# Squares of all norms summed by products in four groups of columns, and x loaded two tiles of channels at a time

## The chip, the core and the metric

The kernel runs on one core of a Trainium2 chip. The metric is the device time of one execution in microseconds. A core has a matrix engine (TensorE, PE in the rows; its weight loads stand apart as PEld), a vector engine (VectorE, DVE), an engine for activations (ScalarE, ACT), a general one (GpSimd, POOL) and SyncE (SP), which issues all the loads and stores here. They run beside each other, each in the order of its own queue, and wait for one another through semaphores. TensorE writes to PSUM, which has eight banks of 128 x 512 floats. Its clock has two levels, 1.2 and 2.4 GHz; the profile shows which one was granted.

## What is computed

Two layers of a backbone over 1024 tokens of 1024 channels: first a convolution layer, then a pooling layer. Both begin with a root-mean-square norm whose result is scaled and shifted, and the first has a layer norm inside. Cut to what matters:

```python
def _rms(x, g):
    y = x * lax.rsqrt(jnp.mean(x * x, axis=-1, keepdims=True) + EPS)
    return y * g

def _conv_mixer(h, w_in, dw, db, ln_g, ln_b, w_out):
    a, b, g = jnp.split(h @ w_in, 3, axis=-1)
    y = a * sigmoid(b)
    y = depthwise_conv(y, dw, width=31) + db
    y = silu(_layernorm(y, ln_g, ln_b)) * silu(g)
    return y @ w_out

# layer 0: convolution mixer, layer 1: pooling mixer
h = _rms(x, norm_g[i]) * (1.0 + sc) + sh
x = x + gt * mixer(h)
```

sh, sc and gt come from the vector c by a product with w_mod.

## The kernel before

Everything is held with the channels on the 128 partitions and the tokens along the row, so a tensor of 1024 x 1024 is eight tiles of channels (KT = 8), each in two halves of 512 tokens (h = 0 and 1). The kernel goes half by half: layer 0 for half 0, then for half 1, with layer 1 of half 0 laid beside the second. All large products are made of three products of fp32r parts (`mm3`, lines 200 to 203: high by high, high by low, low by high), so every weight and every right-hand side is first split into a high part on ACT (line 164 or 165) and a low part on DVE or POOL (line 169 or 170).

There are six norms to which the change belongs: x0 and x1 (the input's two halves, lines 327 to 331), z0 and z1 (the layer norm inside the convolution mixer, `layernorm`, lines 529 to 546), y0 and y1 (the norm before layer 1, summed in `out_half` while it writes the residual, lines 575 to 604, and used in `h2_half`). A norm needs, for each token, the sum of the squares over all channels, which lie on the partitions. Two helpers do it:

- `squares` (line 252; x0, x1 and y1): ACT squares a tile, DVE adds it to a running total of 128 x 512 (line 266), and at the end TensorE takes each block of 128 tokens of the total as its stationary operand and streams one column of ones (line 234). For y1 the last tile of squares isn't added but summed by four products of its own.
- `square_sums` (line 270; z0, z1 and y0): ACT squares a tile, and TensorE takes each of its four blocks of 128 tokens as the stationary operand and streams one column of ones (line 277). The sums of all eight tiles accumulate in one bank, as four columns with the tokens on the partitions.

A tile of squares lives in a ring of two buffers (`sq`), so the third square waits until the first has been summed. `rstd_rows` (line 225) ends the norm: ACT scales the sums by 1/1024 and adds EPS (line 240), POOL raises to the power -0.5 (line 242), ACT makes four diagonal blocks (line 247) and TensorE spreads them over all partitions with a product of ones (line 248, tile `rb`). DVE then multiplies every tile by `rb`.

The convolution has 31 taps. For some tiles of channels DVE does it in PSUM (lines 480 to 489); for two tiles of half 0 and five of half 1 ACT multiplies (line 471, tile `pr`, a ring of two) and POOL adds (line 472).

The gate and modulation vectors of the later steps (`gemv`, line 291) are made by products with 32 columns of weights: four of them fill the four groups of 32 partitions of one bank and are in the array at the same time (line 299). Their result lies in rows 0, 32, 64 and 96 and is turned by a product with `sel`, a selection matrix of 128 x 4 (line 308).

Order: the tile framework lays out each engine's queue when the kernel is built, by a list schedule with priorities and a cost model of its own; `priority(-LATER)` puts work ahead, conv work stands behind, and `behind([...])` makes instructions of a block follow a given instruction in the order of that one's engine. Where a norm is awaited, some projection products are kept back behind the spread product (`HOLD`), so that TensorE has work meanwhile. In the first stage (lines 385 to 421) the loads go in one order by hand: x0 in eight loads, then for each of eight tiles two blocks of w_mod and one of the first weights; DVE takes the modulation from the w_mod blocks by dot products (line 287). They are placed behind `x_done`, the last instruction that `norm_x(0)` issues for the squares. `load_x` writes eight tiles of 128 x 512, two to a unit of 128 x 1024. `out_half` loads the same x again for the residual, in eight loads (line 579).

Of the kernel before, what the change touches and what calls it, by code (L numbers as in the profile page):

```python
# [14 lines left out]
P = 128  # L15
D = 1024
# [37 lines left out]
def hybrid_kernel(ctx, tc, xT, vecs, wm, wk, cv_first, cv_w, cv_wo, pl_w, pl_grp, pl_wo, out):  # L54
# [6 lines left out]
    RINGS = {"w": 4, "raw": 4, "sg": 2, "sq": 2, "pr": 2, "vs": 1}  # L61
# [37 lines left out]
    def hs(h):  # L99
        return slice(h * HW, (h + 1) * HW)  # L100
# [3 lines left out]

    def packed(tags, name):
        res = []
        for j, tag in enumerate(tags):
            u = unit(tag, f"{name}{j}")
            res += [u[:, hs(0)], u[:, hs(1)]]
        return res  # L110
# [114 lines left out]
    def rstd_rows(total, name):  # L225


        sums, vp = total
        if vp is None:
            vp = axps(f"vp{name}")  # L230
            with priority(-LATER):
                for i, summed in enumerate(sums):
                    for j in range(4):
                        nc.tensor.matmul(
                            vp[:, j : j + 1], summed[:, bl(j)], ones[:, 0:1], start=i + j == 0,
                            stop=i == len(sums) - 1, skip_group_check=True,
                        )
        ve = S.tile([P, 4], F32, tag="ve", name=f"ve{name}", bufs=2)
        with priority(-LATER):
            nc.scalar.activation(ve, vp[:, 0:4], AF.Identity, scale=1.0 / D, bias=eps)  # L240
        rs = S.tile([P, 4], F32, tag="vr", name=f"vr{name}", bufs=2)
        power_done[0] = nc.gpsimd.tensor_tensor(out=rs, in0=ve, in1=mhalf[:, 0:4], op=ALU.pow)  # L242
        rb = axps(f"rb{name}")
        dg = half("sq", f"dg{name}")
        with priority(-LATER):
            for j in range(4):
                spread = nc.scalar.activation(dg[:, bl(j)], ident, AF.Copy, scale=rs[:, j : j + 1])
            done = nc.tensor.matmul(rb, ones, dg, start=True, stop=True)  # L248
        spread_done[0] = spread
        return rb, done  # L250

    def squares(xs, name, apart=False):

        total = half("vs", f"va{name}")
        sums = [total]

        def add(i):
            if i == 0:
                nc.scalar.activation(total, xs[i], AF.Square)
                return None  # L260
            sq = half("sq", f"sq{name}{i}")
            nc.scalar.activation(sq, xs[i], AF.Square)
            if apart and i == KT - 1:
                sums.append(sq)
                return None
            return nc.vector.tensor_tensor(out=total, in0=total, in1=sq, op=ALU.add)

        return (sums, None), add

    def square_sums(xs, name, vp):  # L270


        def add(i):
            sq = half("sq", f"sq{name}{i}")
            done = nc.scalar.activation(sq, xs[i], AF.Square)  # L275
            for j in range(4):
                nc.tensor.matmul(  # L277
                    vp[:, j : j + 1], sq[:, bl(j)], ones[:, 0:1], start=i + j == 0, stop=i == KT - 1,
                    skip_group_check=True,
                )  # L280
            return done

        return (None, vp), add
# [38 lines left out]
    def load_x(h):  # L322
        xs[h] = packed([f"{'FZ'[h]}{j}" for j in range(4)], f"x{h}")
        for kt in range(KT):
            load_next(xs[h][kt], xT[bl(kt), hs(h)])

    def norm_x(h):
        total, add = squares(xs[h], f"x{h}")
# [246 lines left out]
    def out_half(h, y1, ws, done, beside=None):  # L575
        group = len(ws)
        x1 = packed([f"Z{j}" for j in range(4)], f"xr{h}")
        for m in range(KT):
            nc.sync.dma_start(out=x1[m], in_=xT[bl(m), hs(h)])
        total, add = squares(x1, f"y{h}", True) if h else square_sums(x1, f"y{h}", axps("vpy0"))  # L580
# [303 lines left out]
```

## Time and profile before

| | us |
|---|---|
| median of 3 runs | 758.52 (757.62 to 759.13) |
| the profiled execution | 758.71 |
| its span, from the first to the last instruction | 756.9 |
| PE busy | 724.2 (96%) |
| PEld busy | 574.1 (76%) |
| DVE busy | 532.1 (70%) |
| POOL busy | 435.4 (58%) |
| ACT busy | 386.4 (51%) |

All times in the rows are microseconds from the start of the span. A matmul's shown duration overlaps that of its neighbours, so the time that products take is read from start to start. Every fp32 matmul stands as two records, an fp32r one as one. A row of the timeline gives start, duration, engine, line, operation, output and inputs, shape and count, and in brackets how long the engine was idle before it and what ended that. Tile names have their buffer numbers left out: vpx, vpz and vpy are the sums of the squares, sqx, sqz and sqy the squares, rbx, rbz and rby the spread results.

### The profile page before, as it was taken

The numbers are of one execution on the slowest core, as the hardware profiler recorded it, in microseconds if no ns is written. First come the engines' busy times: TensorE is split into PE (matmuls) and PEld (weight loads), VectorE is DVE, ScalarE is ACT, GpSimd is POOL, SyncE is SP. The second block draws the span as 40 slices with busy tenths as digits, with TensorE's granted clock in tenths as the row PEclk, the third lists the DMA queues.
The fourth block names the chain that finished last, engine by engine and source line by source line (L and its number), as shares of the span: only waits on it lengthen the run. The fifth ranks groups of instructions, "written<-read, shape, count | busy, mean of one in ns | idle before, by whom it ended". The sixth has DMA issues, their size and how long they took to land.

```text
span 756.9 us, 9894 instructions
## 1 busy us (share of the span) xinstructions
PE 724.2 (96%) x3572; PEld 574.1 (76%) x3572; DVE 532.1 (70%) x724; ACT 386.4 (51%) x576; POOL 435.4 (58%) x377
## 2 busy tenths in 40 slices
PE   3899999999999999999989989999999999999998
PEld 1677786676768788778766768788888788888997
DVE  5997997889898941589969989671737364477321
ACT  5355556656613346876886676652414433334110
POOL 2000889999913438899998999763117413344232
PEclk9999999999999999999999989999999999999999
DMA  8882006466323441643650132445625610334132
GB/s 324 315 318 82 0 1 249 167 223 233 132 82 98 152 153 63 202 140 113 207 171 24 57 126 83 154 168 160 203 92 203 200 56 28 98 112 140 56 126 72
DMA packets 36481, 105.68 MB, mean 140 GB/s; under 512 B 4048, under 2 KB 6224, under 8 KB 36432
## 3 DMA queue, kind: packets, MB, share of 16 engines
q1 hardware_dynamic: 36432, 105.05, 40.8%
q8 instruction: 28, 0.46, 0.2%
q14 instruction: 21, 0.17, 0.1%
HBM read 92.45 MB, written 12.58 MB: 139 GB/s over the span
## 4 chain that ended last, share of the span: by engine, by line
PE 70%; DVE 14%; POOL 8%; ACT 3%; issue 2%; DMA 2%; SPq 0%; DVEq 0%; POOLq 0%; ACTq 0%
POOL z L472 8%; PE ps L201 4%; PE ps L203 4%; PE ps L202 4%; PE psf L202 4%; PE psf L203 4%; PE psf L201 4%; PE psv L203 3%; PE psv L202 3%; PE psv L201 3%; PE psq L202 3%; PE psq L201 3%; PE psq L203 3%; PE psg L203 3%; PE psg L201 3%; PE psg L202 3%
## 5 line engine op out<-in xcount | busy, mean ns | idle before, releaser
L472 POOL TENSOR_TENSOR z<-z,pr 128x512 f32<-128x512 f32 (+8 forms) x210 | 297.1, 1415 | 49.4 <-ACT pr L471 21.2
L471 ACT ACTIVATE pr<-y,VT 128x512 f32<-128x512 f32 (+8 forms) x210 | 150.2, 719 | 96.8 <-POOL z L472 90.2
L484 DVE SCALAR_TENSOR_TENSOR cv<-y,VT,cv 128x512 f32<-128x512 f32 (+12 forms) x261 | 175.4, 741 | 0.4
L770 DVE SCALAR_TENSOR_TENSOR xf<-psf,gt,xf 128x260 f32<-128x260 f32 (+1 forms) x24 | 13.2, 570 | 36.9 <-PE psf L203 31.4
L753 DVE SCALAR_TENSOR_TENSOR q<-psy,VT,q 128x260 f32<-128x260 f32 (+1 forms) x24 | 13.6, 571 | 31.9 <-PE psy L203 31.7
L242 POOL TENSOR_TENSOR vrx<-vex,mhalf 128x4 f32<-128x4 f32 x2 | 2.1, 1026 | 57.2 <-ACT vex L240 57.2
L567 DVE TENSOR_TENSOR z<-z,rbz 128x512 f32<-128x512 f32 x16 | 10.7, 680 | 28.9 <-PE rbz L248 28.9
L671 DVE TENSOR_TENSOR s<-v 128x535 f32<-128x535 f32 x8 | 12.3, 1536 | 19.5 <-ACT v L719 19.5
L675 DVE TENSOR_TENSOR s<-s 128x517 f32<-128x517 f32 (+5 forms) x24 | 20.9, 870 | 0.6
L559 ACT ACTIVATE gn<-z,VT 128x512 f32<-128x512 f32 x16 | 12.4, 777 | 14.6 <-DVE z L567 14.4
L287 DVE SCALAR_TENSOR_TENSOR wmb<-wmb,s_row 128x1024 f32<-128x1024 f32 x16 | 19.4, 1220 | 0.0
L583 DVE SCALAR_TENSOR_TENSOR xr<-pso,gt,xr 128x512 f32<-128x512 f32 x16 | 11.5, 741 | 10.7 <-PE pso L203 10.7
L299 PE MATMUL gv<-wk,srep 128*32 128x256 f32 x256 | 18.6, 388 | 0.0
L164 ACT CAST y<-q 128x504 fp32r<-128x504 f32 (+1 forms) x16 | 9.9, 618 | 16.8 <-DVE q L753 16.8
L169 DVE TENSOR_TENSOR y<-q,y 128x504 fp32r<-128x504 f32 (+1 forms) x16 | 13.9, 869 | 3.6 <-ACT y L164 3.6
L277 PEld LDWEIGHTS vpz<-ones,sqz 128*128 128x128 f32 x128 | 15.5, 191 | 0.7
L275 ACT ACTIVATE sqz<-z 128x512 f32<-128x512 f32 x16 | 9.8, 629 | 12.0 <-PE vpz L277 11.5
L202 PE MATMUL psy<-pd,grs 128*128 128x260 f32 (+1 forms) x48 | 15.3, 320 | 0.0
L203 PE MATMUL psy<-pd,grs 128*128 128x260 f32 (+1 forms) x48 | 15.3, 319 | 0.0
L201 PE MATMUL psy<-pd,grs 128*128 128x260 f32 (+1 forms) x48 | 15.1, 318 | 0.0
L277 PE MATMUL vpz<-ones,sqz 128*128 128x1 f32 x128 | 14.7, 245 | 0.0
L169 DVE TENSOR_TENSOR grs<-gr,grs 128x512 fp32r<-128x512 f32 x8 | 9.1, 1132 | 8.0 <-ACT grs L164 8.0
(2503 smaller groups left out, 2352.6 us busy)
## 6 DMA issues: line engine op xcount, KB each, us to landing
wk<-in_wk SPq DMA_DIRECT2D x32, 512.0 KB, 5.1
wmb<-in_wm SPq DMA_DIRECT2D x16, 512.0 KB, 6.4
wo<-in_cv_wo SPq DMA_DIRECT2D x16, 512.0 KB, 3.5
wp<-in_pl_wo SPq DMA_DIRECT2D x16, 512.0 KB, 3.5
wg<-in_cv_w SPq DMA_DIRECT2D x12, 512.0 KB, 3.7
wv<-in_pl_w SPq DMA_DIRECT2D x12, 512.0 KB, 3.4
wq<-in_pl_w SPq DMA_DIRECT2D x12, 512.0 KB, 3.5
x<-in_xT SPq DMA_DIRECT2D x16, 256.0 KB, 6.2
```

The source lines that it names most:

```text
L169: return eng.tensor_tensor(out=lo, in0=src, in1=hi.bitcast(F32), op=ALU.subtract)
L201: nc.tensor.matmul(ps, w[0], r[0], start=first, stop=False)
L202: nc.tensor.matmul(ps, w[0], r[1], start=False, stop=False)
L203: nc.tensor.matmul(ps, w[1], r[0], start=False, stop=last)
L277: nc.tensor.matmul(vp[:, j : j + 1], sq[:, bl(j)], ones[:, 0:1], start=i + j == 0, stop=i == KT - 1, skip_group_check=True,)
L287: nc.vector.scalar_tensor_tensor(out=w, in0=w, scalar=1.0, in1=s_row, op0=ALU.mult, op1=ALU.mult, accum_out=out)
L299: nc.tensor.matmul(ps[32 * q : 32 * q + 32, :256], srep[:, kt, :], w[:, 256 * q : 256 * q + 256], start=kt == 0, stop=kt == KT - 1,)
L471: nc.scalar.activation(pr[:, o], y[:, i], AF.Copy, scale=dw(k))
L472: nc.gpsimd.tensor_tensor(out=z[:, o], in0=z[:, o], in1=pr[:, o], op=ALU.add)
L484: nc.vector.scalar_tensor_tensor(out=a[:, o], in0=y[:, i], scalar=dw(k), in1=a[:, o], op0=ALU.mult, op1=ALU.add)
L675: nc.vector.tensor_tensor(out=s[:, :m], in0=s[:, :m], in1=s[:, step : step + m], op=ALU.add)
L753: mixed[0] = nc.vector.scalar_tensor_tensor(out=sg[m][:, piece], in0=ps, scalar=vcol(ct, V_PS), in1=sg[m][:, piece], op0=ALU.mult, op1=ALU ...
```

## The change

All six norms now use `square_sums`, and its products are turned round: for each of the four blocks of 128 tokens the stationary operand is 32 columns of `onesd` (all 1/1024) and the squares are streamed, 128 columns, into one of the four groups of 32 partitions (`token_sums`). The bank then holds, in each group, the mean of squares of 128 tokens along the row. `rstd_rows` copies this 128 x 128 block to SBUF on ACT with EPS added, turns it with a product with `sel` into four columns, copies these on ACT, and goes on as before; the power on POOL now stands inside the priority block. `squares`, its running total and the DVE adds are gone. What `norm_x` returns as the last instruction is now the last square on ACT, where it was the last add on DVE.

x is laid out anew in memory, so that one load of 128 rows of 4 KB brings two tiles of channels of one half: `load_x` and `out_half` make four loads of 512 KB each where they made eight of 256 KB.

```diff
-    def rstd_rows(total, name):
-        sums, vp = total
-        if vp is None:
-            vp = axps(f"vp{name}")
-            with priority(-LATER):
-                for i, summed in enumerate(sums):
-                    for j in range(4):
-                        nc.tensor.matmul(
-                            vp[:, j : j + 1], summed[:, bl(j)], ones[:, 0:1], start=i + j == 0,
-                            stop=i == len(sums) - 1, skip_group_check=True,
-                        )
-        ve = S.tile([P, 4], F32, tag="ve", name=f"ve{name}", bufs=2)
+    def token_sums(ps, src, first, last):
+        for j in range(4):
+            nc.tensor.matmul(ps[32 * j : 32 * j + 32, :P], onesd[:, :32], src[:, bl(j)], start=first, stop=last)
+
+    def rstd_rows(vp, name):
+        row = S.tile([P, P], F32, tag="vrow", name=f"vrow{name}", bufs=1)
+        rs = S.tile([P, 4], F32, tag="vr", name=f"vr{name}", bufs=2)
         with priority(-LATER):
-            nc.scalar.activation(ve, vp[:, 0:4], AF.Identity, scale=1.0 / D, bias=eps)
-        rs = S.tile([P, 4], F32, tag="vr", name=f"vr{name}", bufs=2)
-        power_done[0] = nc.gpsimd.tensor_tensor(out=rs, in0=ve, in1=mhalf[:, 0:4], op=ALU.pow)
+            nc.scalar.activation(row, vp[:, :P], AF.Identity, bias=eps)
+            nc.tensor.matmul(vp[:, P : P + 4], row, sel, start=True, stop=True)
+            ve = S.tile([P, 4], F32, tag="ve", name=f"ve{name}", bufs=2)
+            nc.scalar.copy(ve, vp[:, P : P + 4])
+            power_done[0] = nc.gpsimd.tensor_tensor(out=rs, in0=ve, in1=mhalf[:, 0:4], op=ALU.pow)
...
-    def squares(xs, name, apart=False):
...
     def square_sums(xs, name, vp):
         def add(i):
             sq = half("sq", f"sq{name}{i}")
             done = nc.scalar.activation(sq, xs[i], AF.Square)
-            for j in range(4):
-                nc.tensor.matmul(
-                    vp[:, j : j + 1], sq[:, bl(j)], ones[:, 0:1], start=i + j == 0, stop=i == KT - 1,
-                    skip_group_check=True,
-                )
+            token_sums(vp, sq, i == 0, i == KT - 1)
             return done
-        return (None, vp), add
+        return vp, add
...
     def load_x(h):
-        xs[h] = packed([f"{'FZ'[h]}{j}" for j in range(4)], f"x{h}")
-        for kt in range(KT):
-            load_next(xs[h][kt], xT[bl(kt), hs(h)])
+        xs[h] = []
+        for j in range(4):
+            u = unit(f"{'FZ'[h]}{j}", f"x{h}{j}")
+            load_next(u, xT[h, j])
+            xs[h] += [u[:, hs(0)], u[:, hs(1)]]
 
     def norm_x(h):
-        total, add = squares(xs[h], f"x{h}")
+        total, add = square_sums(xs[h], f"x{h}", axps(f"vpx{h}"))
...
     def out_half(h, y1, ws, done, beside=None):
-        x1 = packed([f"Z{j}" for j in range(4)], f"xr{h}")
-        for m in range(KT):
-            nc.sync.dma_start(out=x1[m], in_=xT[bl(m), hs(h)])
-        total, add = squares(x1, f"y{h}", True) if h else square_sums(x1, f"y{h}", axps("vpy0"))
+        x1 = []
+        for j in range(4):
+            u = unit(f"Z{j}", f"xr{h}{j}")
+            nc.sync.dma_start(out=u, in_=xT[h, j])
+            x1 += [u[:, hs(0)], u[:, hs(1)]]
+        total, add = square_sums(x1, f"y{h}", axps(f"vpy{h}"))
...
-        "xT": g["x"][0].T,
+        "xT": g["x"][0].T.reshape(4, 2, P, 2, HW).transpose(3, 0, 2, 1, 4).reshape(2, 4, P, 2 * HW),
```

## Rows read from the trace of the kernel before

**Rows 1.** The page's busy times: busy us, share, instructions of each engine.
```profile
PE 724.2 (96%) x3572; PEld 574.1 (76%) x3572; DVE 532.1 (70%) x724; ACT 386.4 (51%) x576; POOL 435.4 (58%) x377
```

**Rows 2.** Waits of TensorE: who waited for whom, us in total, times, longest.
```profile
PE psv L203 <- DVE wv40l L169: 3.7, 1, 3.7
...
PE pg L202 <- DVE h10l L170: 1.2, 1, 1.2
```

**Rows 3.** Timeline of TensorE around two tiles of z0's squares.
```profile
267.83 0.39 PE L203 MATMUL psg<-h16h,wg00l 128*128 128x512 f32 x1
268.06 1.84 PE L277 MATMUL vpz<-ones,sqz 128*128 128x1 f32 x16
269.76 0.48 PE L201 MATMUL psg<-h00h,wg20h 128*128 128x512 f32 x1
270.08 0.39 PE L202 MATMUL psg<-h00l,wg20h 128*128 128x512 f32 x1
```

**Rows 4.** Timeline of TensorE and ACT at the end of y0's norm.
```profile
372.67 0.95 PE L277 MATMUL vpy<-ones,sqy 128*128 128x1 f32 x8
373.48 0.48 PE L203 MATMUL psg<-h12h,wg61l 128*128 128x512 f32 x1
...
378.84 0.24 ACT L240 ACTIVATE vey<-vpy,eps 128x4 f32<-128x4 f32 x1
...
382.49 1.13 PE L248 MATMUL rby<-dgy,ones 128*128 128x512 f32 x2 [0.74 <-ACT dgy L247]
```

**Rows 5.** Timeline of TensorE around four tiles of a modulation vector's product.
```profile
147.73 0.39 PE L203 MATMUL ps<-h16h,wa4l 128*128 128x512 f32 x1
148.05 1.93 PE L299 MATMUL gv<-wk,srep 128*32 128x256 f32 x32
149.91 0.50 PE L201 MATMUL ps<-h00h,wb5h 128*128 128x512 f32 x1
150.25 0.40 PE L202 MATMUL ps<-h00l,wb5h 128*128 128x512 f32 x1
```

**Rows 6.** Timeline of ACT in the start: the end of x0's norm.
```profile
15.69 0.27 ACT L240 ACTIVATE vex<-vpx,eps 128x4 f32<-128x4 f32 x1 [2.95 <-PE vpx L234]
...
17.19 1.28 ACT L247 ACTIVATE dgx<-ident,vrx 128x128 f32<-128x128 f32 x4 [0.29 <-POOL vrx L242]
...
22.03 0.72 ACT L165 ACTIVATE h00h<-x,sh 128x512 fp32r<-128x512 f32 x1 [0.81 <-DVE x L366]
```

**Rows 7.** Groups by line: busy us, mean ns | idle before: adds for x0, x1.
```profile
L266 DVE TENSOR_TENSOR vax<-vax,sqx 128x512 f32<-128x512 f32 x14 | 9.6, 688 | 3.3 <-ACT sqx L262 2.9
```

**Rows 8.** Windows: stretch, length, busy us of each engine, PEclk, DMA share, GB/s.
```profile
11.50:19.00 7.50, 2.35 (x9) 2.27 (x10) 6.64 (x11) 3.69 (x9) 1.04 (x1) 1.00 1.02 418
...
8.00:11.50 3.50, 0.74 (x1) 0.00 (x0) 2.19 (x4) 3.20 (x7) 0.00 (x0) 1.00 1.00 368
```

**Rows 9.** Timeline of TensorE: two products with sel of a modulation vector.
```profile
141.74 0.50 PE L308 MATMUL gv<-sel,row 128*128 128x4 f32 x4
```

**Rows 10.** Timeline of DVE where it waits for the first gates.
```profile
65.08 1.29 DVE L382 TENSOR_TENSOR y<-pf,sig 128x512 f32<-128x512 f32 x2 [3.62 <-ACT sig L381]
```

**Rows 11.** Timeline of ACT and POOL: z0's last square, POOL's second half.
```profile
283.04 0.63 ACT L275 ACTIVATE sqz<-z 128x512 f32<-128x512 f32 x1 [0.26 <-PE vpz L277]
...
285.07 2.66 POOL L472 TENSOR_TENSOR z<-z,pr 128x512 f32<-128x512 f32 x2 [13.47 <-ACT pr L471]
```

**Rows 12.** Windows (columns as in rows 8): PE, PEld, DVE, ACT, POOL busy.
```profile
390.00:444.00 54.00, 51.60 (x217) 38.43 (x217) 54.00 (x65) 38.73 (x61) 49.54 (x53) 1.00 0.22 73
...
448.40:453.80 5.40, 5.36 (x13) 4.21 (x14) 1.97 (x3) 4.13 (x7) 5.24 (x7) 0.50 0.45 146
```

**Rows 13.** Timeline of ACT and TensorE at the end of y1's norm.
```profile
593.82 0.63 ACT L262 ACTIVATE sqy<-xr 128x512 f32<-128x512 f32 x1 [0.20 <-DVE xr L583]
...
598.70 0.95 PE L234 MATMUL vpy<-ones,sqy 128*128 128x1 f32 x8
...
602.78 1.02 PE L248 MATMUL rby<-dgy,ones 128*128 128x512 f32 x2
```

More of the change, by code (lines that the diff above doesn't have):

```diff
@@ L59, in hybrid_kernel @@
     DR = ctx.enter_context(tc.tile_pool(name="dr", bufs=1, space=bass.MemoryType.DRAM))
-    RINGS = {"w": 4, "raw": 4, "sg": 2, "sq": 2, "pr": 2, "vs": 1}
+    RINGS = {"w": 4, "raw": 4, "sg": 2, "sq": 2, "pr": 2}
     WIDTH = {"E": 2 * NB, "Z": 2 * (NB + 2 * PAD), "sg": NB + 2 * PAD, "pr": NB}
@@ L103, in bl @@
         return slice(j * P, (j + 1) * P)
[L105 to L110, printed above, removed]
     def pair(region, i, name):
@@ L250, in rstd_rows @@
         return rb, done
-    def squares(xs, name, apart=False):
[L254 to L268, printed above, removed]
     def square_sums(xs, name, vp):
```

## The prediction

> **What bounds the kernel now.** I read the busy shares first: TensorE is busy 96% of the span [rows 1], so the time is the sum of its work, its start, and the few places where it waits. The list of waits names those places: the longest after the start is 3.7 us on a weight split of DVE, another 1.2 us on h10l [rows 2]. Then I read the timeline of TensorE around each kind of product that the change touches, to get the step from one start to the next, because a matmul's shown duration overlaps its neighbour's. Last I read ACT and POOL around the norms, where the chain of waits leaves TensorE: POOL's convolution paces the stretch from 285 to 390 us, DVE the one after it.
>
> The profiled execution took 758.71 us (span 756.9 and 1.8 around it), 0.2 above the median of the runs; the sum is made against 758.71.
>
> **The price of the sums.** A projection product starts 0.23 us after the one before [rows 3]. Two tiles of squares (16 records) start at 268.06, the next product at 269.76, the one after at 270.08. From 267.83 to 270.08 is 2.25, less two ordinary steps (0.46): 1.79 us a pair [rows 3]. That is a price of loading 128 columns of weights for each pass, since only one column is then streamed. A lone tile takes 0.81 from start to start, 0.90 with its edge [rows 4]. z0 and z1 have four pairs each (14.3), y0 two pairs and four lone tiles (7.2), x1 one group of four products (0.9), y1 two such groups (2.0). All this goes.
>
> The new form (32 columns of weights, four groups beside each other) is what the gate vectors do with 256 streamed columns: 32 records, four tiles, from 147.73 to 150.25 are 2.52, less 0.46: 2.06 us [rows 5]. Eight steps of 256 columns in it; the start-to-start of one such step, by (149.91 - 148.05) / 8, is at most 0.23 and, without the way out of the mode, 0.216 (an estimate: 2 x 256 columns at the 2.4 GHz level). So 2.06 = 8 x 0.216 + 0.33 for going in and out. With 128 columns, a tile has two steps. If they scale with columns: 2 x 0.108 + 0.33 = 0.55 lone, 0.76 a pair. If a step can't be shorter than with 256 columns: 0.77 and 1.20. I take the first, since the same rows show all groups of one step side by side and the step as long as its columns; the second is kept for the range. The clock stood at its full level in these rows.
>
> At this place a rule of the Trainium skill speaks against the change. The page "TensorE: Matmul & The Clock Gate", section "Wait — 56ns, not 53.3ns?", gives a floor of about 25 ns between matmul starts, and about 62 ns where microcode decodes them. By the first, eight records need 0.20 us and nothing changes; by the second they need 0.50 in place of 0.22, and the 40 tiles below would make the sum 11 us larger, 765.6. The rows leave little room for the second: 32 records in 1.86 us are 58 ns each, under 62, but not by much, and with fewer columns none of them can tell.
>
> **The change, part by part.**
> - *Start.* Today ACT has been idle for 2.95 us when it takes up the variance at 15.69 [rows 6], so the last square ended at 12.74; between lie an add of DVE (0.69 [rows 7]) and eight slow records. New: the x loads have 4 KB rows. While x was landing the queues moved 368 GB/s, then 418 with 4 KB rows only [rows 8]: 2 MB would land 0.3 to 0.6 us sooner, and the squares no longer wait for DVE to free their ring: last square at about 12.4. Then, as estimates from twice the prices above, the four groups at the lower clock level (0.45, plus about 0.3 to drain and signal), the row on ACT (0.32, a quarter of the 1.28 for four of 128x128 [rows 6]), the product with sel (twice 0.25 and a hand-over, 0.6), the copy (0.27): the variance is out at 14.55 against 15.96. POOL's power, the spread and everything up to h00h at 22.03 follow unchanged: **-1.4** (-0.5 to -2.0).
> - *x1.* TensorE gets eight tiles, as pairs since the ring of squares has two: 4 x 0.76 = 3.05, and one product with sel. Four records of that kind take at most 0.50 [rows 9], so 0.25 each. Less 0.90: **+2.4** (to +4.2 if they come singly). DVE loses seven adds, 4.6 to 4.8 us of the 9.6 [rows 7], in a stretch where it is full. Later it idles 3.62 us for the first gates [rows 10]; with the norm of x1 done sooner, the multiplications with it can fill that hole, and the wait of 1.2 us for h10l [rows 2] with its neighbours goes: **-1.5** (0 to -2.5).
> - *z0.* 4 x (1.79 - 0.76) less 0.25: **-3.85**. It also moves POOL: the seventh and eighth square wait on ACT for the sums of the pair before (0.26 idle at 283.04, released by vpz), and POOL's second half, idle for 13.47 us, starts at 285.07 behind them [rows 11]. Three pairs are ahead of that, so it starts about 3 us sooner.
> - *y0.* TensorE saves 7.2 - (2 x 0.76 + 4 x 0.55) - 0.25 = 3.2. But the stretch is paced by POOL and DVE (DVE 54.0 us busy of 54 from 390 to 444, and TensorE waits at its end [rows 2, 12]), so a sooner TensorE waits longer there: **0** (-3.2 to +5, below). The norm's end gets one more visit to ACT and one to TensorE, covered by the gate products held ready.
> - *z1.* As z0: **-3.85**. There TensorE waits for nothing and the norm's end has filler products behind it.
> - *y1.* In the output projection TensorE gets two pairs and four lone tiles, 3.7, and 0.25, less 2.0: **+2.0**. The six adds on DVE that go were beside TensorE's work and free nothing. The end is a chain: last square begun 593.82, sums 598.70, spread product 602.78 [rows 13]; between them stand exactly the products kept back for it. New links: row 0.32, sel 0.25, copy, and TensorE's place for sel. Today a finished square waits about 4.2 us for its place (594.45 to 598.70). From 1 us (sel taken at once) to 4.2 (the same queueing again); I take **+1.9**, as the kept-back products run out by then.
> - Reloading x in the output halves as four loads each: they land long before they are used; 0. The removed tile and scaling of ACT: 0.
>
> Sum: -1.4 + 2.4 - 1.5 - 3.85 + 0 - 3.85 + 2.0 + 1.9 = -4.3, so 754.4.
>
> **Rivals.**
> 1. *The stall stays away altogether.* With DVE freed early, its first convolution and so z0's norm may come sooner, and then POOL's second half, by more than the 3 us. If TensorE no longer stops at 444 us, 3.7 us of waiting and the slow stretch behind it (5.4 us at a granted 0.50, its 1.2 GHz level [rows 12], 2.7 lost) go, and y0's 3.2 pass: 754.4 - 9.6 = 744.8, with half of it 749.6. For it: POOL stood idle for 13.47 us. Against: DVE is full before that wait, and POOL's convolution is not shortened. Chance 0.19.
> 2. *The pace swallows it.* If POOL's start is set by something other than the squares, z0's 3.85 is absorbed as well: 758.3, no change. Chance 0.16.
> 3. *Slower: the product with sel blocks TensorE in y0.* TensorE runs in order. After y0's last sums (373.48) ACT took the variance only at 378.84, because multiplications for POOL stand ahead in its queue [rows 4]. Now the row goes through that queue, then sel on TensorE, then the copy through the queue again. Where sel stands among the gate products is set in advance; with fewer than about 23 of them (5.3 us / 0.23) ahead, TensorE stops for the rest, and the clock can fall as at 448. Up to 5.3 + 2.7: 762.4. Against: the spread product shows only 0.74 us of idle [rows 4], so the order knows of slow ACT. Chance 0.17.
> 4. *Slower: 128 columns are no cheaper than 256.* 40 tiles x 0.216 = 8.6: 763.0. Chance 0.10. The bound of 62 ns on the page "TensorE: Matmul & The Clock Gate" of the Trainium skill is a case by itself, 765.6, with a chance of 0.04.
> 5. *It isn't what it says:* groups run one after another, 0.65 more for each of 40 tiles, 780. The gate rows show them together: 0.01.
>
> **How the numbers follow.** Forecast 754.4, chance 0.33, its own range 751.5 to 757.5. About 0.2% (1.5 us) is what a measurement here can tell from no change. Faster: the forecast (0.32 of it) and rival 1, together 0.51; same: rival 2 and slips, 0.18; slower: rivals 3 to 5, 0.31. The range takes in rival 3 and the bound of 256 columns, and leaves out the lower half of rival 1 and what lies above 4: 747.0 to 763.5. The order of all instructions is laid out anew when one is changed, which can move stalls of 1 to 4 us [rows 2] either way; that is within it.
>
> **What would show it.** In the timeline after: the sums of a pair of z at 0.76 us instead of 1.79 (1.20: rival 4). The first projection product at about 21.4 instead of 22.8. No wait for h10l. POOL's second half starting at about 281. The wait at 444 still there and longer. In y0 a wait of TensorE on the row: rival 3. In y1 the spread product 3 to 6 us later behind the last output product. The prediction falls if those prices are right and the waits of TensorE add up to more than today's.

## The result, and the profile after

The changed kernel takes 770.18 us (median; 769.26 to 770.79) where the kernel before took 758.07 beside it: ratio 1.0157, interval 1.0139 to 1.0175. It is 12 us slower where 4 us faster was forecast. The profiled execution took 769.65, its span is 767.6 for 756.9.

The busy times and the longest waits of TensorE (engine, line, waited for: us in total, times, longest) of the kernel after:

```profile
PE 725.1 (94%) x3744; PEld 559.5 (73%) x3744; DVE 512.7 (67%) x704; ACT 388.0 (51%) x582; POOL 433.5 (56%) x377
...
PE rby L239 <- ACT dgy L238: 7.2, 2, 4.6
PE rbx L239 <- ACT dgx L238: 4.6, 1, 4.6
...
PE psv L196 <- DVE wv40l L162: 3.8, 1, 3.8
PE pg L195 <- DVE h10l L163: 3.5, 1, 3.5
PE pso L194 <- ACT y102h L157: 2.0, 2, 1.0
```

DVE is busy 19.4 us less than before [rows 1], and the time doesn't show it. TensorE is hardly busier (725.1 us for 724.2), its share fell from 96% to 94%, and the time stands in waits that were not there, or were short: for the spread product of the y norms (7.2 where it was 0.7), in the start for that of x0 (4.6 where it was 2.9), for h10l (3.5 where it was 1.2 [rows 2]), for the operands y100h to y103l of the first output products (4.5 in all, 2.0 of it for y102h, where it was 1.0). So the sums are not what became dear. TensorE's timeline after, around a pair of z0's tiles and one lone tile of y1, shows that they cost what was forecast (in this and the later timelines the rows that don't bear on the point are left out):

```profile
272.60 0.39 PE L196 MATMUL psg<-h16h,wg00l 128*128 128x512 f32 x1
272.91 0.64 PE L222 MATMUL vpz<-sqz,onesd 128*32 128x128 f32 x16
273.49 0.50 PE L194 MATMUL psg<-h00h,wg20h 128*128 128x512 f32 x1
273.82 0.39 PE L195 MATMUL psg<-h00l,wg20h 128*128 128x512 f32 x1
...
599.75 0.39 PE L195 MATMUL psf<-y,wp60h 128*128 128x504 f32 x1
600.07 0.42 PE L222 MATMUL vpy<-sqy,onesd 128*32 128x128 f32 x8
600.42 0.50 PE L196 MATMUL psf<-y,wp60l 128*128 128x504 f32 x1
600.76 0.39 PE L194 MATMUL psf<-y,wp60h 128*128 128x504 f32 x1
```

Read as in [rows 3]: from 272.60 to 273.82 are 1.22, less two ordinary steps (0.46), 0.76 us a pair where it was 1.79. From 599.75 to 600.76 are 1.01, less 0.46: 0.55 for a lone tile. Both are the forecast's figures.

Where the time went can be followed along TensorE, by the start of the first product with some weight tile in either trace (after minus before): first projection product -0.3; first with h10h (74.39) +1.3; second stage of weights (124.05) +4.8; wg30, behind three of the four pairs of z0's sums (291.71), -0.1; wo04, behind the first output products of half 0 (335.12), +5.7; wv40 (451.62) +7.5; wo10, first output product of half 1 (551.87), +4.4; wo17 (594.00) +7.7; we01, behind y1's norm (617.07), +10.7, and from there to the end the same. The two z norms do give what they were to give: 4.9 us up to wg30, of which 0.8 is there only because the last pair of z0's sums now stands behind wg30, so 4.1; and 3.2 us from wv40 to wo10 for z1. Four places take it away: x1, z0, y0 and y1. All four lie at the end of a norm, but for 3.4 us of y1's, which lie in the output products ahead of it. The first of them, x1, in TensorE's and ACT's timeline after, with two rows of before at the end:

```profile
57.30 0.64 PE L222 MATMUL vpx<-sqx,onesd 128*32 128x128 f32 x14
57.99 0.37 ACT L229 ACTIVATE vrowx<-vpx,eps 128x128 f32<-128x128 f32 x1 [1.26 <-PE vpx L222]
63.06 0.28 PE L230 MATMUL vpx<-sel,vrowx 128*128 128x4 f32 x2
63.37 0.16 ACT L232 COPY vex<-vpx 128x4 f32<-128x4 f32 x1 [5.01 <-PE vpx L230]
64.68 1.27 ACT L238 ACTIVATE dgx<-ident,vrx 128x128 f32<-128x128 f32 x4
70.54 1.02 PE L239 MATMUL rbx<-dgx,ones 128*128 128x512 f32 x2
74.39 1.09 PE L194 MATMUL pg<-h10h,w00h 128*128 128x512 f32 x4
78.96 0.60 PE L195 MATMUL pg<-h10l,w00h 128*128 128x512 f32 x1 [3.47 <-DVE h10l L163]
...
63.29 1.28 ACT L247 ACTIVATE dgx<-ident,vrx 128x128 f32<-128x128 f32 x4 [1.12 <-POOL vrx L242]
66.66 1.02 PE L248 MATMUL rbx<-dgx,ones 128*128 128x512 f32 x2
```

The row is in SBUF at 58.36, but the product with sel starts at 63.06, 4.7 us later, while TensorE works on projection products that stand ahead of it. Its result is used at once: ACT sat idle 5.01 us for it. The diagonals are done at 65.95, and the spread product starts at 70.54: another 4.6 us behind other products. The links themselves (0.37, 0.28, 0.16, the power's 1.0, 1.27) are as short as forecast. The new visit to TensorE costs not 0.25 us but its place in the queue. The same holds at z0 and z1, and in part at the y norms (us from the operand being there to the product's start, from the timelines; z0's spread product before is shown below the table):

| norm | before: spread | after: sel | after: spread |
|---|---|---|---|
| x1 | 2.1 | 4.7 | 4.6 |
| z0 | 4.7 | 4.4 | 5.1 |
| z1 | 4.3 | 4.4 | 4.2 |
| y0 | 0.1, after 0.74 idle [rows 4] | 1.9 | 0.1, after 4.60 idle |
| y1 | 0.4 | 2.1 | 0.1, after 2.65 idle |

```profile
292.53 1.27 ACT L247 ACTIVATE dgz<-ident,vrz 128x128 f32<-128x128 f32 x4
298.51 1.02 PE L248 MATMUL rbz<-dgz,ones 128*128 128x512 f32 x2
```

At the y norms the kept-back products run out and TensorE stands still, and the clock falls behind each such wait. TensorE's rows of both spread products after, and the windows of what follows (stretch, length, busy us of PE, PEld, DVE, ACT and POOL, then the granted clock):

```profile
393.32 2.07 PE L239 MATMUL rby<-dgy,ones 128*128 128x512 f32 x2 [4.60 <-ACT dgy L238]
...
611.79 2.08 PE L239 MATMUL rby<-dgy,ones 128*128 128x512 f32 x2 [2.65 <-ACT dgy L238]
...
79.20:82.60 3.40, 3.40 (x9) 2.62 (x9) 3.40 (x6) 1.08 (x2) 0.19 (x1) 0.50 0.02 5
393.20:396.60 3.40, 3.28 (x6) 1.96 (x7) 1.17 (x2) 2.40 (x5) 2.78 (x3) 0.50 0.14 54
...
611.70:615.10 3.40, 3.31 (x6) 2.01 (x7) 1.20 (x2) 1.39 (x3) 2.30 (x1) 0.50 0.00 0
```

0.50 is the lower level, 1.2 GHz; each of the three stretches of 3.4 us costs about 1.7 us of work, an estimate from the level alone. None of the three is there before, where the clock was lowered behind the wait for wv40l only [rows 12]. The clock stood at 0.50 in the start as well, from 14.3 to 28.0, and before it didn't. That stretch costs little: from the first projection product to the first with h10h TensorE took 50.30 us before, and 50.29 and 50.56 in two traces with x0 and x1 in their old form and a stretch at 0.50 up to 25.0 and 28.0 (y0 alone changed, and the kernel before with its places fixed, both below).

### The profile page after: what moved, and what is told of

It reads as the page before. It is cut to its first block, busy times and chain, and to the rows that moved or that the text cites. A ratio compares the mean times of both kernels' runs of the same rounds, so it can differ in the third digit from the quotient of the medians.

```text
span 767.6 us, 10199 instructions
## 1 busy us (share of the span) xinstructions
PE 725.1 (94%) x3744; PEld 559.5 (73%) x3744; DVE 512.7 (67%) x704; ACT 388.0 (51%) x582; POOL 433.5 (56%) x377
## 4 chain that ended last, share of the span: by engine, by line
PE 79%; POOL 9%; ACT 4%; DVE 4%; issue 2%; DMA 1%; SPq 0%; POOLq 0%; ACTq 0%
POOL z L443 8%; PE ps L194 4%; PE ps L196 4%; PE ps L195 4%; PE psf L195 4%; PE psv L196 4%; PE psf L196 4%; PE psf L194 4%; PE psv L194 4%; PE psv L195 4%; PE psq L196 3%; PE psq L194 3%; PE psq L195 3%; PE psg L194 3%; PE psg L195 3%; PE psg L196 3%
## 5 line engine op out<-in xcount | busy, mean ns | idle before, releaser
L538 DVE TENSOR_TENSOR z<-z,rbz 128x512 f32<-128x512 f32 x16 | 10.7, 679 | 26.2 <-PE rbz L239 26.1
L648 DVE TENSOR_TENSOR s<-s 128x517 f32<-128x517 f32 (+5 forms) x24 | 25.5, 1063 | 0.6
L644 DVE TENSOR_TENSOR s<-v 128x535 f32<-128x535 f32 x8 | 12.3, 1538 | 19.5 <-ACT v L692 19.5
L256 DVE SCALAR_TENSOR_TENSOR wmb<-wmb,s_row 128x1024 f32<-128x1024 f32 x16 | 19.4, 1221 | 6.2 <-DMA wmb<-in_wm 6.1
L587 DVE SCALAR_TENSOR_TENSOR xr<-xr,a,rby 128x512 f32<-128x512 f32 x16 | 11.7, 738 | 14.0 <-PE rby L239 14.0
L530 ACT ACTIVATE gn<-z,VT 128x512 f32<-128x512 f32 x16 | 12.3, 774 | 13.2 <-DVE z L538 13.2
L460 DVE TENSOR_TENSOR z<-z,cv 128x512 f32<-128x512 f32 x9 | 6.1, 682 | 11.8 <-ACT z L459 11.8
L451 DVE TENSOR_SCALAR cv<-y,VT 128x512 f32<-128x512 f32 (+1 forms) x18 | 12.8, 748 | 1.4 <-ACT z L459 1.3
```

The source lines that it names most:

```text
L256: nc.vector.scalar_tensor_tensor(out=w, in0=w, scalar=1.0, in1=s_row, op0=ALU.mult, op1=ALU.mult, accum_out=out)
L648: nc.vector.tensor_tensor(out=s[:, :m], in0=s[:, :m], in1=s[:, step : step + m], op=ALU.add)
```

## The experiments

Two theories stood at first. H: the longer end of the norms is what costs. W: what costs is the products that the sums of x1 and y1 bring to TensorE. Two rivals stood beside them. L: the new loads cost it. G: the order of all instructions, laid out anew, costs it, and no norm by itself.

**The longer end alone.** The kernel before, with one more product (with the unit matrix) and one more copy on ACT in each norm; the sums as they were.

```diff
             nc.scalar.activation(ve, vp[:, 0:4], AF.Identity, scale=1.0 / D, bias=eps)
+            nc.tensor.matmul(vp[:, 8:12], ident, ve, start=True, stop=True)
+            ve = S.tile([P, 4], F32, tag="ve2", name=f"vf{name}", bufs=2)
+            nc.scalar.copy(ve, vp[:, 8:12])
```

> The kernel before, with one thing added: at the end of each of the six norms the variance goes once more through TensorE (a product of 128x128 with 4 columns) and is copied back on ACT before the power. Sums, loads and additions stay as before. Theory H (the longer end of each norm makes TensorE run out of the products kept back for it): TensorE waits for the spread product in y0 (about 5 us) and in y1 (about 3 us), for h10l after x1 (2 us more than before), and its clock drops after the waits; 766 to 772 us. Theory W (the changed kernel is slower for the products that x1 and y1 bring to TensorE): six products of 0.23 us are all that is added, 758 to 760 us.

775.80 us, ratio 1.0233 (1.0217 to 1.0248). H has the direction, and its 766 to 772 us are too little. Six products of 0.3 us and six copies of 0.16 us, under 3 us together, cost 18 us. x1 in its trace, as above:

```profile
61.96 0.26 ACT L240 ACTIVATE vex<-vpx,eps 128x4 f32<-128x4 f32 x1 [1.24 <-PE vpx L234]
66.50 0.28 PE L241 MATMUL vpx<-vex,ident 128*128 128x4 f32 x2
67.28 0.16 ACT L243 COPY vfx<-vpx 128x4 f32<-128x4 f32 x1
68.56 1.28 ACT L250 ACTIVATE dgx<-ident,vrx 128x128 f32<-128x128 f32 x4 [0.62 <-POOL vrx L245]
72.53 1.02 PE L251 MATMUL rbx<-dgx,ones 128*128 128x512 f32 x2
```

The variance is there at 62.22, as before; the added product starts 4.3 us later, the spread product 5.9 us later than the 66.66 of before. The added work alone can't be 18 us; whether it is the places of the added products or the new order as a whole, this run doesn't tell.

**Without the extra visit.** The changed kernel, with the power taken on the whole 128 x 128 block on POOL and the spread made by four products with a selection matrix, so that the product with sel and the copy go.

> The changed kernel with a shorter end of each norm: ACT adds EPS to the 128x128 block, POOL raises the whole block to the power -0.5, and TensorE spreads it with four products of 128x128 selection matrices into rb; the product with sel, the copy and the four diagonal blocks fall away. Group sums, squares and loads stay as changed. Theory H: the waits for the spread product in y0 and y1 go; what is left is the cheaper sums (z0 and z1 8 us, y0 2.6) against the added products of x1 and y1 (2.2 and 2.4): 748 to 757 us. Theory W: the loss stays, 766 to 771 us. A power on 128x128 that takes POOL over 5 us would hide H's gain; its duration is read from the trace.

866.30 us, ratio 1.1429: it doesn't separate the theories, since POOL's power now takes 20 times as long (POOL's timeline, x0's power):

```profile
14.13 21.02 POOL L234 TENSOR_TENSOR vrowx<-vrowx,mhalf 128x128 f32<-128x128 f32 x1 [8.74 <-ACT vrowx L233]
```

**x and y1 added on DVE again.** The changed kernel, but the squares of x0, x1 and y1 are added by DVE, and the total alone goes through one set of group products; the new norm end stays everywhere (its block now lies in a buffer that the gate vectors' rows use too, here and in the runs on one norm).

```diff
-        total, add = square_sums(xs[h], f"x{h}", axps(f"vpx{h}"))
+        total, add = added_sums(xs[h], f"x{h}", axps(f"vpx{h}"))
...
-        total, add = square_sums(x1, f"y{h}", axps(f"vpy{h}"))
+        total, add = (added_sums if h else square_sums)(x1, f"y{h}", axps(f"vpy{h}"))
```

> The changed kernel, but for x0, x1 and y1 the squares are added by DVE as before and only the total is summed, by one set of four group products. The new end of the norms stays. Theory W: the loss is in the products of x1 and y1, so most of it goes: 757 to 762 us. Theory H: x1's and y1's longer ends stay, y0's and z0's too; only about 4 us of products go, 764 to 769 us.

758.71 us, ratio 1.0009 (0.9998 to 1.002): as W had it. But its trace bears W out only in part. The output products of half 1 take 38.8 us from wo10 to wo17 as before, for 42.1 with y1's sums on TensorE; that much is W's. At x1, though, the places changed too. In this order the product with sel of x1 happens to start 1.2 us behind its row, and the spread product 1.2 us behind its diagonals:

```profile
56.45 0.37 ACT L229 ACTIVATE vrowx<-vpx,eps 128x128 f32<-128x128 f32 x1 [1.58 <-PE vpx L222]
58.04 0.28 PE L230 MATMUL vpx<-sel,vrowx 128*128 128x4 f32 x2
59.86 1.29 ACT L238 ACTIVATE dgx<-ident,vrx 128x128 f32<-128x128 f32 x4 [1.34 <-POOL vrx L233]
...
62.37 1.02 PE L239 MATMUL rbx<-dgx,ones 128*128 128x512 f32 x2
```

Sums and places changed at once there, so the run alone can't decide between them. At the y norms the waits for the spread products stay (7.3 us in all).

**Old loads.** The changed kernel with x in its old layout and eight loads a half.

> The changed kernel with x laid out and loaded as before (eight loads of 256 KB for each half, rows of 2 KB). Theory L (the loads are part of the loss: the first tile comes later): 2 us or more faster than the changed kernel, under 768 us. Theories H and W: 769.5 to 771.5 us, no difference beyond 0.2%.

770.66 us, ratio 1.0170 (1.0153 to 1.0187), for 1.0157 with the new loads: no difference beyond the intervals. L falls.

**One norm at a time.** Five runs put the new sums and the new end into the kernel before for some norms only (old loads; `NEW` holds the names):

```diff
+NEW = ('z1',)
...
+            if name in NEW:
+                token_sums(vp, sq, i == 0, i == KT - 1)
+                return done
```

> The kernel before, with the new sums and the new norm end for x0 and x1 alone. Theory P (each norm changes the time at its own place, and the places add up): the full change was 4.8 us late at the first product with half 1 of the input's second weight stage (about 119 us), so 762 to 765, with a wait of TensorE of about 3.5 us for h10l and a stretch at half clock behind it. Rival G (the loss comes from the order of all instructions being laid out anew, and from no norm by itself): 758 to 760, or any time that the milestones of the full change do not give. The prediction's terms for x0 and x1 (start -1.4, x1 +2.4 - 1.5) would give 757.6.

> The kernel before, with the new sums and the new norm end for z0 alone. P: the gain of 3.9 to 4.9 us on TensorE is there before the first gate product that follows the sums, and is given back where the first output products wait for z0's spread product, which is 5 to 8 us later: 757 to 760. G: nothing in particular; a wait in another norm. The prediction's term for z0: 754.2.

> The kernel before, with the new sums and the new norm end for z1 alone. P: the sums cost TensorE 3.9 us less, and in the full change 3.1 us of it were still there when the output products of half 1 began; nothing of the norm's end shows, since the kept-back products cover it: 754 to 755.5. G: within 1 us of the kernel before. The prediction's term for z1: 754.2.

> The kernel before, with the new sums and the new norm end for y1 alone. P: in the full change 6.3 us were lost between the start of the output products of half 1 and the first product behind y1's spread product (3.4 in the output stage, the rest at the end of the norm with a stretch at half clock): 762 to 765. G: 758 to 760. The prediction's term for y1 (+2.0 + 1.9): 762.0.

> The kernel before, with the new sums and the new norm end for y0 alone, the last of the parts. The other four, each alone, changed the median by +7.2, +1.5, -0.5 and +6.1 (14.3 together) where all together change it by 12.1. P (places add up): TensorE waits 3 to 5 us for y0's spread product and the clock falls behind it; the full change loses 1.9 us between the output products of half 0 and the weight wv40: 758 to 761. If the parts add up to the last digit it would be 755.5 to 756, and the norm's longer end at y0 would be a gain, which nothing in the traces supports. The prediction's term for y0: no change.

| new form in | us | before beside it | ratio (interval) |
|---|---|---|---|
| x0 and x1 | 764.91 | 757.74 | 1.0093 (1.0076 to 1.0110) |
| z0 | 759.24 | 757.74 | 1.0019 (1.0010 to 1.0028) |
| y0 | 760.30 | 757.24 | 1.0035 (1.0022 to 1.0049) |
| z1 | 757.24 | 757.74 | 0.9994 (0.9984 to 1.0003) |
| y1 | 763.79 | 757.74 | 1.0078 (1.0063 to 1.0093) |

x, z0, y0 and y1 each lose alone, in the expected range and at the place where the full change loses, so the loss isn't a chance of the order as a whole: G falls there. Of P the places hold, but not the sum: the parts add up to 17 us, 5 more than the whole. Some of it is x's start (the first projection product stands at 24.59, for 22.48 in the full change and 23.40 in the full change with old loads); the rest isn't settled. z1 was expected at 754 to 755.5 and brought 0.5, which isn't clear of noise and is the figure that G had: in its trace the output products begin 4.0 us sooner (0.4 of it is the start), but 1.9 of that is lost in the last of them, which waits 2.2 us for a weight split of POOL (0.5 before). z0 shows most plainly where a gain goes. TensorE's timeline with z0 alone changed:

```profile
292.11 0.28 PE L249 MATMUL vpz<-sel,vrowz 128*128 128x4 f32 x2
...
300.60 1.02 PE L263 MATMUL rbz<-dgz,ones 128*128 128x512 f32 x2
...
305.03 0.50 PE L202 MATMUL pso<-y100h,wo00h 128*128 128x512 f32 x1 [0.45 <-ACT y100h L165]
...
307.94 0.50 PE L202 MATMUL pso<-y100h,wo00h 128*128 128x512 f32 x1 [0.53 <-ACT y100h L165]
```

The output products begin at 305.03 where they began at 309.27, but the spread product is at 300.60 for 298.51, and what hangs on it (y100h and its fellows) now comes too late: TensorE waits for tile after tile, 4.5 us in all, and at wo04 it stands where it stood before, though this execution's start was 1.0 us shorter.

**The places in the queue fixed by hand.** Theory Q: a link of a norm's end costs what it takes plus the products that stand ahead of it, about 4 us a visit, and the new end has two visits for one. The test adds and removes no work: projection products are told to follow the product with sel, or the spread product. An entry (k, i) in `place` puts the products from step k on behind instruction i:

```diff
         for kt in range(KT):
-            with behind(after if kt >= start else ()):
+            with behind([*(after if kt >= start else ()), *(i for k, i in place if kt >= k)]):
...
-    layer1_out(0, range(MID_OUT - 1), ahead, group)
+    place += [(6, sel_mm[0]), (7, spread_mm[0])]
+    layer1_out(0, range(MID_OUT - 2), ahead, group)
+    place[:] = [(0, spread_mm[0])]
+    layer1_out(0, [MID_OUT - 2])
+    place.clear()
```

This is z1; x1, z0 and y1 have their like (y1 also for its last sums; for z0 one gate product is written behind the norm).

> The changed kernel, with the places of sel's product and of the spread product in TensorE's queue fixed by hand for x1, z0, z1 and y1: some projection products are issued behind them (for y1 also behind the last sums), so that they start when their operand is ready and not 4 us later. No work is added or removed. Theory Q (a step of the norm's end costs what it takes plus the products that stand ahead of it in TensorE's queue, about 4 us a visit, and the new end has two visits for one): the spread products come 4 to 8 us sooner at x1, z0 and z1, and 3 to 5 sooner at y1, and the time falls to 757 to 764. Theory W (what costs is the sums' own products on TensorE at x1 and y1, and waits for the squares): 767 to 770, with the waits moved.

> The kernel before with the new form for z1 alone, and the places of sel's product and the spread product fixed by hand: three ordinary products between the last sums' neighbours and sel, twelve between sel and the spread product, where the order by itself had 21 and 31. Q: the spread product of z1 comes at about 529 instead of 534.9, TensorE keeps the 3.9 us that the sums leave it, and the end of the kernel is 3.5 to 4 us earlier than before: 753.5 to 755. If the 1.9 us that the version without fixed places lost in the output stage have another cause (POOL's splits): 756 to 757.5.

> As the run beside it (z1 new, places fixed), and the places of y1's last sums and spread product fixed as well, with y1's sums in their old form. Q: y1's chain from the last square to the spread product gets 2 to 3 us shorter, but TensorE doesn't wait there in the kernel before, so this alone brings nothing: the same as the run beside it within 1 us.

The changed kernel so ordered takes 751.98 us (749.77 to 755.66), ratio 0.9936 (0.9914 to 0.9958): 18 us less than the same work in the framework's order, and faster than the kernel before. The execution in the trace took 755.66, so the trace can show 14 of the 18. x1 and z1 in it:

```profile
57.43 0.37 ACT L234 ACTIVATE vrowx<-vpx,eps 128x128 f32<-128x128 f32 x1 [1.26 <-PE vpx L225]
58.80 0.28 PE L235 MATMUL vpx<-sel,vrowx 128*128 128x4 f32 x2
60.39 1.28 ACT L243 ACTIVATE dgx<-ident,vrx 128x128 f32<-128x128 f32 x4 [1.12 <-POOL vrx L238]
62.47 1.02 PE L244 MATMUL rbx<-dgx,ones 128*128 128x512 f32 x2
74.29 0.39 PE L195 MATMUL pg<-h10l,w00h 128*128 128x512 f32 x1
...
523.35 0.37 ACT L234 ACTIVATE vrowz<-vpz,eps 128x128 f32<-128x128 f32 x1 [1.38 <-PE vpz L225]
524.01 0.28 PE L235 MATMUL vpz<-sel,vrowz 128*128 128x4 f32 x2
526.98 1.09 PE L244 MATMUL rbz<-dgz,ones 128*128 128x512 f32 x2
```

x1's spread product comes 8.1 us sooner (62.47 for 70.54), and there is no wait for h10l at all; z1's comes 3.6 us after the row is begun, where that took 12.3. Q was expected at 757 to 764 and does better, though not every place moved: at z0 the spread product stands 1.9 us behind its diagonals for 5.1, but sel still 4.4 behind its row; at y1 the last sums stand 1.5 us behind their square for 4.7, but sel 2.6 behind its row for 2.1. Along TensorE the trace gains 5.8 us on the changed kernel up to the second stage of weights, 4.1 more up to wo04, 1.7 up to wv40, and 3.6 between wo17 and we01; from wv40 to wo10 it loses 1.2. The 1.7 are at y0, whose places weren't fixed: its wait of 4.60 is 0.5 here, and TensorE waits 3.1 for y0's last square instead. So the new order as a whole has a part in the 18 us as well. The clean cases are one norm at a time. With z1 alone changed and placed: 754.01 (0.9956, 0.9941 to 0.9971), where it was 757.24 without the places, so 3.2 of the forecast's 3.85 us are there once the end comes in time. Fixing the old y1 as well: 753.51, the same within a us, as expected.

**Whose gain is it?** Three more runs: the kernel before with its own places fixed, the changed kernel with x1 alone placed, and the placed one with y1's squares added on DVE.

> The kernel before with its old sums and old norm end, and the places of the spread products of x1, z1 and y1 and of y1's last sums fixed by hand in the way that took 18 us off the changed kernel. Theory S (the change saves TensorE work and its longer norm end is harmless where it is placed well; fixed places help the new end because it has one visit more): 755 to 758, so the placed changed kernel stays 3 to 6 us faster than this. Rival T (the fixed places are worth as much to the old form; the change itself is worth nothing): 750 to 753.5.

> The changed kernel with the places fixed at x1 alone, all else in the framework's own order. If the places at the norms act each by itself, the 4.8 us that the changed kernel is late at 119 us, and with them the wait for h10l and the half clock behind it, go, but the later norms lose what they lost: 764 to 766. If x1's delay is what the later stages wait for: 757 to 761. If the sums' products at x1 cost the time: 769 to 771.

> The changed kernel with fixed places (751.98 in its first runs), but y1's squares are added on DVE as before and the total alone is summed by four group products. In the run with fixed places the output products of half 1 take 3.4 us longer than before (42.1 for 38.8 from the first to the last weight), which is what eight lone tiles cost TensorE. If that is the last loss of the change, this gives 748 to 750; if DVE's adds come late for the norm's end, as in the kernel before, 751 to 754.

The kernel before gains 1.5 us from it: 756.19, ratio 0.9979 (0.9970 to 0.9988). So S holds: fixed places are worth 18 us to the new end and 1.5 to the old one. The edit names z0's spread product too, but in the trace it still starts 4.7 us behind its diagonals, so three spread products and y1's last sums moved, and T was not tried at z0. x1 alone placed: 764.46 (762.51 to 765.31), 5.7 less than the change, the expected size; the later norms keep their losses. With y1 on DVE: 749.60 us (749.01 to 751.17), ratio 0.9891 (0.9876 to 0.9905), the fastest of all. In its trace the output products of half 1 take 38.8 us from wo10 to wo17 as before, for 42.1 with the sums on TensorE, and TensorE doesn't stand before y1's spread product, only 1.45 us before the sums:

```profile
586.59 0.42 PE L225 MATMUL vpy<-vay,onesd 128*32 128x128 f32 x8 [1.45 <-DVE vay L269]
588.42 0.28 PE L235 MATMUL vpy<-sel,vrowy 128*128 128x4 f32 x2
592.31 1.02 PE L244 MATMUL rby<-dgy,ones 128*128 128x512 f32 x2
```

So W is the smaller part: 3.4 us in this stage, 2.4 between the medians, whose runs overlap (749.01 to 751.17 and 749.77 to 755.66). At x1 TensorE does the sums of all eight tiles in the placed kernel too, and reaches the second stage of weights 1 us ahead of the kernel before; x1's squares added on DVE with its places fixed was not run.

## Why the prediction was wrong, by its own steps

- **The price of the sums** was right to the hundredth: 0.76 and 0.55. Rivals 4 and 5 fall with it. In the pair 16 records take 0.58 us from the first start to the next product's, 36 ns each on average; within it the four records of a step start some 7 ns apart, and the steps 109 to 133 ns apart. The Trainium skill's page "TensorE: Matmul & The Clock Gate", section "Wait — 56ns, not 53.3ns?", gives floors of about 25 ns between starts and of about 62 ns per product where microcode decodes it; 36 ns on average is under the second, and 7 ns under both, so by this trace neither bounds products in different groups.
- **Start, -1.4:** measured -0.3 in this pair of traces, and no gain over all of them: the first projection product starts at 21.69 to 22.80 in the eight traces with x0 in its old form and the old loads, of which before is the latest, and at 22.48 to 23.26 in the four with both new. The variance was out at 14.73, for a forecast of 14.55 (the terms listed there add up to 14.34). It was late because the copy's operand was there at 13.61, but ACT took a cast of w00h at 13.63 and the copy only behind it, at 14.58. Then POOL's power took 1.94 us where it had taken 1.04. The step that failed is "follow unchanged".
- **x1, +2.4 and -1.5:** the products cost +1.6 up to the first with h10h, less than forecast. The second term had the wrong sign. It took the norm of x1 to be done sooner since DVE is freed; the last sums were indeed sooner (57.30 for 60.92), but the spread product came 3.9 us later, and the wait for h10l grew from 1.2 to 3.5 with the half clock behind it: together +3.5 from the first product with h10h to the second stage of weights. Fixing x1's places alone brought 5.7 us.
- **z0, -3.85:** the gain is in the trace (4.1 at the prices measured) and was lost at the output products, which the step doesn't name: it counts TensorE's work and POOL's start, and leaves the later spread product out. POOL's second half did not start 3 us sooner either: with z0 alone changed it starts at 283.71 for 285.07, and 1.0 of this is the start.
- **y0, 0:** "covered by the gate products held ready" failed. TensorE waited 4.60 us for the spread product, with the lower clock behind it; alone the norm costs 3.1 us. Rival 3 had the norm and the mechanism right, a wait of up to 5.3 us and the clock behind it (2.7 there, about 1.7 here), but looked for the wait at the product with sel. That one came when its operand had been there for 1.9 us; the copy behind it then waited 2.4 us for its turn on ACT (388.91), and the wait ended up at the spread product.
- **z1, -3.85:** right in size, 3.2 us at the first output product of half 1 (3.7 alone, less its start); "filler products behind it" held for TensorE's waits, but the queue place cost 4.4 and 4.2 us here as well, and alone the norm brought 0.5.
- **y1, +2.0 and +1.9:** measured +3.4 in the output stage and +3.0 at the end. All tiles came singly, where the prediction had two pairs; six of them lie in the output stage, and none of the old sums did: they lay behind it, and the prediction set the whole of their price against the new ones. At the end the last sums stood 4.7 us behind their square (4.2 before), then sel 2.1, then TensorE stood still for 2.65 us and lost about 1.7 to the clock.
- **Rivals 1 and 2:** the wait for wv40l is still there with its 3.8 us, so 1 falls. 2 had it right that z0's gain is swallowed, but not by POOL's pace: by the spread product, as the waits for y100h show.
- **The sum.** Terms that were prices of work held, but for y1's pairs. Terms that were waits were set at nothing or at a fraction of the right size, because the prediction took a link's cost for its duration wherever TensorE had other work. [Rows 13] had the evidence: a finished square of y1 waited 4.2 us for its place. It was read for y1 alone, and the same 4 us stand before the spread products of z0 and z1. Why the framework sets such products some 20 places late, the traces don't show. That fixing the place gives the time back, x1 (5.7 us) and z1 (3.2) show one at a time; for z0 and y1 it is shown only in the run that fixes all four norms, and y0's places were fixed in none.

## What to carry to other kernels

Before a link is added to a chain across engines, read from the trace how long an operand that is ready waits for its place on the engine that takes it: that wait, more than the link's duration, is its price (here 4 to 5 us at x1, z0 and z1), and it can be paid at every visit. That an engine is busy all the time doesn't make a short link free: find out what waits for the chain's end, and whether the work kept back for that time lasts for the longer chain. Where the order is laid out by a schedule, fixing the places of a few small products can be worth more than the change itself, here 18 us against the 4.3 that the forecast gave the change.

## What the hardware showed that was not expected

- POOL's power takes 1.02 us on 128 x 4 and 20.7 us on 128 x 128: 32 times the elements, 20 times the time, 0.16 us a column in the large one. On 128 x 4 it took 1.94 in the start of the changed kernel, where it took 1.04 in that of the kernel before, and 1.46 at z1 after; why isn't shown.
- In fp32, products of 128 columns in four groups of 32 partitions start some 7 ns apart, and the next four 109 to 133 ns behind them. Two tiles cost 0.76 us and one 0.55, so a tile costs about 0.21 and going into and out of this form about 0.34 a time.
- TensorE was granted 0.50 of its clock for 3.4 us behind waits of 2.65, 3.47 and 4.60 us, for 6.8 us behind the wait for wv40l, and for 13.7 us in the start, where that cost little.
